# A two-layer retention and attention trunk: first stage in eight steps of 128 features, gates multiplied in the third group

## The chip, the cores and the metric

The kernel runs on one NeuronCore of a Trainium2 chip. The metric is the device time of one execution in microseconds (us); the time of a kernel is the median of its runs. The engines are TensorE (PE in the profile; its weight loads are PEld), VectorE (DVE), ScalarE (ACT), GpSimd (POOL) and SyncE (SP), which issues most loads. An engine works through its own queue in order.

## What is computed

One sequence of 512 tokens with 1024 features goes through two layers. Both begin with an RMS norm and a modulation from a condition vector, and end with a gated residual:

```python
cond = silu(c)
mod = cond @ ada_w[i] + ada_b[i]                 # 3 x 1024: shift, scale, gate
h = rms_norm(x, norm_g[i]) * (1 + scale) + shift
out = retention_mixer(h, ...) if i == 0 else chunked_attention_mixer(h, ...)
x = x + gate * out
```

Layer 0 (retention): `h @ w_in` gives q, k (4 heads of 256), v and a gate branch g (4 heads of 512); q and k are rotated by the positions (rope); scores with a decay, times v, RMS norm per head, times silu(g), then `@ w_out`. Layer 1 (attention): 16 heads of 128, RMS-normed q and k, softmax with a relative bias, times silu(g), then `@ w_out`. All is float32.

## The kernel before, in words

**Precision.** A float32 product is made of three fast ones: each operand is split into a high part (ScalarE, `AF.Copy` into float32r) and the rest (VectorE, source less high part); TensorE adds high x high, high x low and low x high. `split` (L305) does this for activations, `load` (L204) for weights: one load of 512 rows in a tile `raw`, the high part `whi`, the rest `wlo`. `nat_mm` (L226) and `tr_mm` (L235) issue the three matmuls for each 128 rows, with tokens or with features on the output's partitions.

**Condition and modulation.** `c_row` is loaded broadcast to 128 partitions (L76) and put through silu (L99). The 24 blocks of 128 rows of `ada_w` of a layer are loaded transposed; `ada_dot` (L123) takes the dot product of each row with the condition on VectorE (1024 columns at once). `ada_finish` (L128) adds the bias and makes the shift `sh`, the scale `gs`, or the gate: for the gate it spreads each value over the partitions by a product of a diagonal matrix with ones on TensorE (`diag` L145, `gp` L146) into `gates[layer]`.

**First stage (L348 to L398).** `norm_x` loads four x tiles of 128 tokens, normalises them (`norm_rows` L163: two squares on ScalarE, the mean and the power -0.5 on GpSimd in `rstd_of` L114, the scaling on VectorE, for the last tile on ScalarE), transposes them on TensorE and copies them to `xT`. `prepare(s)`, for four steps of 256 features, loads four blocks of `ada_w`, makes shift and scale, h on VectorE (L379) and its split, and loads and splits the weights of `first`: v of head 0 (rv0) and q of head 0 (rqk0_0), two thirds of head 0's q, k, v in all. The products of step s are issued behind `prepare(s + 1)`, into six accumulators of PSUM (pools `pm` and `pa`, four buffers each). The last step's products are issued behind `rope_tables` (L421), which makes `cos` and `sin` with some 14 operations on VectorE and two on ScalarE from the positions, loaded over GpSimd's queue (L423) into a buffer of the pool tag `nat`, which the h tiles of the stage use too. Then k of head 0 (rqk0_2) is a chunk of its own.

**The rest.** Work is cut into units of twelve matmuls of 512 columns. `go` (L294) issues units; `at` (L291) hangs other work behind a unit number: loads and dots of the remaining `ada_w` blocks (`side_load`, `side_dot`, L587 to L605: first the gate of layer 0 in units 2 to 16, then layer 1), scores and mixes (`hang_scores`, `hang_mix`). For each head of layer 0 come q and k, v, g; `out_proj` (L310) multiplies 512 features of the result with rows of `w_out` in four groups (`outp(0)` to `outp(3)`; a0 to a3 in layer 1). It scales the weights with the gate on GpSimd when they are loaded (L219, tile `raw_r` or `raw_a` of 512 rows by 512 columns) and adds the product to `xs` on VectorE (L327, L324). Behind the last group of layer 0 `done` (L629) hangs `norm_tile` (L184), the norm of layer 1. In the end the last group of layer 1 stores the result.

The order of each engine's queue is made by the tile framework's planner from the program's order and its own estimates, not written out by hand; `keep_in_program_order` pins the side loads and dots, `high_priority` the first silu.

## Time and profile before

| | us |
|---|---|
| median of 3 runs | 984.57 |
| the three runs | 982.72, 984.57, 985.76 |
| the profiled execution | 982.98 |
| its span in the profile | 981.2 |

Some 1.8 us of the profiled execution lie around its span. In a timeline a row gives the start, the duration, the engine, the line of the kernel, the operation with the tiles written and read, and in brackets how long the engine had idled and what released it. Matmuls are pipelined, so the distance between their starts is what one costs, not the printed duration. Short operations of VectorE overlap their neighbours in the same way.

### The profile page before, as it was taken

The page shows a single profiled execution, that of the slowest core. Times are in us where ns is not written, and L with a number is a line of the kernel's source. Part 1 is how long each engine was busy: PE and PEld are TensorE (multiplying, and loading weights), DVE is VectorE, ACT ScalarE, POOL GpSimd, SP SyncE. Part 2 cuts the span into 40 slices and gives each one's busy share as a digit, 9 for nine tenths or more (in the row PEclk, how much of TensorE's full clock was granted, in tenths as well). Part 3 has the DMA queues.
Part 4 walks back from the last instruction along what each step waited for, and adds up shares of the span by engine and source line. Part 5 has one row for each costly group of instructions (what it writes and reads, how often), then busy time and mean ns, then how long its engine had stood idle before and what let it go on. Part 6 is the DMA issues. An engine that isn't in the chain of part 4 may idle for free.

```text
span 981.2 us, 11783 instructions
## 1 busy us (share of the span) xinstructions
PE 949.3 (97%) x4528; PEld 793.6 (81%) x4528; DVE 601.1 (61%) x1023; ACT 373.8 (38%) x785; POOL 184.7 (19%) x169
## 2 busy tenths in 40 slices
PE   3889999999999999999999999999999999999997
PEld 2778888888888888778788888888878888888886
DVE  4977796568544775864455557444676346555674
ACT  6233322232233233354444445233543244444441
POOL 3000520051002012503001250002520012004410
PEclk8899999999999999999999999999999999999999
DMA  9654436434443433312333213223212232223202
GB/s 352 241 191 160 149 99 204 151 108 140 150 150 108 150 100 104 97 57 80 101 97 97 79 62 103 91 87 96 97 58 93 87 97 90 79 70 99 95 1 86
DMA packets 70296, 111.76 MB, mean 114 GB/s; under 512 B 11888, under 2 KB 36512, under 8 KB 70240
## 3 DMA queue, kind: packets, MB, share of 16 engines
q1 hardware_dynamic: 58256, 103.29, 31.5%
q0 software_dynamic: 10832, 5.62, 2.1%
q10 hardware_dynamic: 1152, 2.10, 0.6%
q8 instruction: 35, 0.57, 0.2%
q14 instruction: 21, 0.17, 0.1%
HBM read 108.83 MB, written 2.10 MB: 113 GB/s over the span
## 4 chain that ended last, share of the span: by engine, by line
PE 86%; DMA 4%; issue 4%; DVE 3%; ACT 1%; POOL 1%; SPq 0%; POOLq 0%; ACTq 0%; DVEq 0%
PE pm_aqk L233 5%; PE pm_aqk L231 5%; PE pm_aqk L232 5%; PE po_a L231 3%; PE po_a L233 3%; PE po_a L232 3%; PE pm_av L232 3%; PE pm_av L233 3%; PE pm_rg L239 3%; PE pm_rg L240 3%; PE ao L765 3%; PE as L725 3%; PE pm_av L231 3%; PE pm_rg L241 3%; PE ro L540 3%
## 5 line engine op out<-in xcount | busy, mean ns | idle before, releaser
L231 PE MATMUL pm_aqk<-whi_aqk,hTh 128*128 128x512 f32 x256 | 102.3, 400 | 1.1 <-ACT hTh L200 1.1
L233 PE MATMUL pm_aqk<-whi_aqk,hTl 128*128 128x512 f32 x256 | 100.4, 393 | 0.0
L232 PE MATMUL pm_aqk<-wlo_aqk,hTh 128*128 128x512 f32 x256 | 100.2, 391 | 0.0
L124 DVE CUSTOM_DVE_ANT_0 ada<-ada,cond 128x1024 f32<-128x1024 f32 x48 | 63.3, 1332 | 1.7 <-DMA ada<-in_ada_t_dram 1.7
L219 POOL TENSOR_TENSOR raw_r<-raw_r,gate 128x2048 f32<-128x2048 f32 x8 | 38.2, 4771 | 106.3 <-DMA raw_r<-in_ret_w_out_dram 92.9
L231 PE MATMUL pm_rv<-whi_rv,hTh 128*128 128x512 f32 x128 | 51.2, 407 | 6.7 <-ACT hTh L306 6.7
L231 PEld LDWEIGHTS pm_aqk<-whi_aqk,hTh 128*128 128x128 f32 x256 | 48.1, 188 | 10.9 <-ACT hTh L200 1.5
L233 PEld LDWEIGHTS pm_aqk<-whi_aqk,hTl 128*128 128x128 f32 x256 | 48.1, 188 | 10.6 <-DVE hTl L201 0.4
L232 PEld LDWEIGHTS pm_aqk<-wlo_aqk,hTh 128*128 128x128 f32 x256 | 48.2, 188 | 9.2
L734 ACT ACTIVATE p<-p,nm 128x128 f32<-128x128 f32 (+1 forms) x64 | 35.9, 563 | 48.7 <-DVE nm L732 47.6
L223 DVE TENSOR_TENSOR wlo_aqk<-raw_aqk,whi_aqk 128x2048 fp32r<-128x2048 f32 x16 | 36.6, 2290 | 28.0 <-ACT whi_aqk L222 28.0
L728 DVE CUSTOM_DVE_ANT_0 p<-as,br 128x128 f32<-128x128 f32 (+1 forms) x64 | 30.4, 486 | 36.9 <-PE as L725 34.0
L241 PE MATMUL pm_rqk<-hTh,wlo_rqk 128*128 128x512 f32 x128 | 49.7, 391 | 2.5 <-DVE wlo_rqk L223 2.5
L713 POOL DMA_DIRECT2D br<-in_att_bias_dram x16 | 13.4, 839 | 204.4 <-DVE nm L732 168.8
L232 PE MATMUL pm_rv<-wlo_rv,hTh 128*128 128x512 f32 x128 | 50.9, 402 | 0.0
L239 PE MATMUL pm_ag<-hTh,whi_ag 128*128 128x512 f32 x128 | 50.7, 397 | 0.0
L240 PE MATMUL pm_ag<-hTl,whi_ag 128*128 128x512 f32 x128 | 50.5, 394 | 0.0
L231 PE MATMUL po_r<-whi_r,yh 128*128 128x512 f32 x128 | 49.8, 391 | 0.5 <-ACT whi_r L222 0.5
L241 PE MATMUL pm_ag<-hTh,wlo_ag 128*128 128x512 f32 x128 | 50.2, 395 | 0.0
L233 PE MATMUL po_r<-whi_r,yl 128*128 128x512 f32 x128 | 50.1, 392 | 0.0
L232 PE MATMUL po_r<-wlo_r,yh 128*128 128x512 f32 x128 | 50.0, 391 | 0.0
L231 PE MATMUL pm_av<-whi_av,hTh 128*128 128x512 f32 x128 | 50.0, 391 | 0.0
(199 smaller groups left out, 2548.6 us busy)
## 6 DMA issues: line engine op xcount, KB each, us to landing
ada<-in_ada_t_dram SPq DMA_DIRECT2D x32, 512.0 KB, 4.4
raw_aqk<-in_att_w_in_dram SPq DMA_DIRECT2D x32, 512.0 KB, 4.6
ada<-in_ada_t_dram SPq DMA_DIRECT2D x8, 1024.0 KB, 13.8
raw_rg<-in_ret_w_in_dram SPq DMA_DIRECT2D x8, 1024.0 KB, 5.1
raw_r<-in_ret_w_out_dram SPq DMA_DIRECT2D x8, 1024.0 KB, 5.0
raw_ag<-in_att_w_in_dram SPq DMA_DIRECT2D x8, 1024.0 KB, 5.2
raw_av<-in_att_w_in_dram SPq DMA_DIRECT2D x8, 1024.0 KB, 5.1
raw_a<-in_att_w_out_dram SPq DMA_DIRECT2D x8, 1024.0 KB, 4.9
```

What stands on the lines that cost most here:

```text
L124: return nc.vector.tensor_tensor_reduce(raw, raw, cond, 1.0, 0.0, ALU.mult, ALU.add, mod[:, layer, block : block + 1])
L219: nc.gpsimd.tensor_tensor(raw, raw, scale.unsqueeze(1).broadcast_to([P, k1 - k0, width]), ALU.mult)
L223: nc.vector.tensor_tensor(lo, raw, f32(hi), ALU.subtract)
L231: nc.tensor.matmul(ps, a_h, wh[:, k, :], start=first and k == 0, stop=False)
L232: nc.tensor.matmul(ps, a_h, wl[:, k, :], start=False, stop=False)
L233: nc.tensor.matmul(ps, a_l, wh[:, k, :], start=False, stop=last and k == 3)
L239: nc.tensor.matmul(ps, wh[:, k, csl], h, start=first and k == 0, stop=False)
L240: nc.tensor.matmul(ps, wh[:, k, csl], l, start=False, stop=False)
L241: nc.tensor.matmul(ps, wl[:, k, csl], h, start=False, stop=last and k == 3)
L540: nc.tensor.matmul(ps[:, S - w :], a[:, fsl], b[:, psl], start=j == 0 and z == 0, stop=j == 3 and z == 2,)
L728: nc.vector.tensor_tensor_reduce(p[:, :w], ps[:, :w], br[:, S - w :], 1.0, -3.0e38, ALU.add, ALU.max, mx)
L734: nc.scalar.activation(p[:, :w], p[:, :w], AF.Exp, bias=nm, accum_out=sm)
```

## The change

What it does:

- The condition is loaded to one partition (ScalarE's queue), put through silu there, spread to 128 partitions by a matmul with ones, and copied back; a silu on a small tile `tick` stands ahead. The x tiles are first on SP's queue; the two small tables `ng` and `bt` move from GpSimd's queue to ScalarE's.
- `norm_rows` makes one of the two squares of the first norm on VectorE; the mean and epsilon are two small VectorE operations, only the power stays on GpSimd; all scaling is on VectorE.
- The first stage has eight steps of 128 features, holds v, q and k of head 0 in eight accumulators, makes h on ScalarE, adds the shift's bias on GpSimd, and has the rope tables behind its third step. The separate chunk of k is gone.
- The gate: groups 0 to 2 use unscaled weights. Group 0 writes `xs` (ScalarE), group 1 adds, group 2 adds, multiplies the sum with the gate and adds x, which it loads again (`again`). Group 3 has gate-scaled weights as before. For layer 1, `done` stores layer 0's result to a DRAM tile `x1` over GpSimd's queue. The dots of the side blocks are spread over units 4 to 93, and some work is hung two units later.

```diff
+    x1 = dp.tile([S, D], F32, name="x1")
...
-    nc.sync.dma_start(cond, c_row.broadcast_to([P, D]))
+    nc.scalar.dma_start(cond[0:1, :], c_row)
     xs = [cp.tile([P, D], F32, name=f"x_{t}") for t in range(NT)]
+    for t in range(NT):
+        nc.sync.dma_start(xs[t], x[t * P : (t + 1) * P, :])
...
     with tc.high_priority():
-        nc.scalar.activation(cond, cond, AF.Silu)
+        nc.scalar.activation(tick, tick, AF.Silu)
+    nc.scalar.activation(cond[0:1, :], cond[0:1, :], AF.Silu)
+    for half in range(2):
+        csl = slice(half * 512, (half + 1) * 512)
+        ps = pm.tile([P, 512], F32, tag="pm", name=f"cp_{half}")
+        nc.tensor.matmul(ps, ones[0:1, :], cond[0:1, csl], start=True, stop=True)
+        nc.scalar.activation(cond[:, csl], ps, AF.Copy)
...
-    def norm_rows(t, tag, scalar=False):
+    def norm_rows(t, tag, vector=False):
...
+            if vector and half:
+                nc.vector.tensor_tensor_reduce(
+                    xh, src, src, 1.0, 0.0, ALU.mult, ALU.add, ss[:, half : half + 1]
+                )
+            else:
+                nc.scalar.activation(xh, src, AF.Square, accum_out=ss[:, half : half + 1])
...
-        s1 = sp.tile([P, 16], F32, tag="s1", name=f"s1_{tag}_{t}")
-        nc.vector.tensor_tensor(s1[:, 0:1], ss[:, 0:1], ss[:, 1:2], ALU.add)
-        rs = rstd_of(s1[:, 0:1], D, 1)
+        ms = sp.tile([P, 2], F32, tag="s1", name=f"s1_{tag}_{t}")
+        nc.vector.tensor_scalar(ms[:, 0:1], ss[:, 0:1], 1.0 / D, EPS, ALU.mult, ALU.add)
+        nc.vector.scalar_tensor_tensor(
+            ms[:, 1:2], ss[:, 1:2], 1.0 / D, ms[:, 0:1], ALU.mult, ALU.add
+        )
+        rs = sp.tile([P, 1], F32, tag="rs", name="rs")
+        nc.gpsimd.tensor_tensor(rs, ms[:, 1:2], mhalf[:, 0:1], ALU.pow)
...
-    def out_proj(name, w_out, row0, ys, gate, store=None, t_outer=False, done=None, rstd=None):
+    def out_proj(name, w_out, row0, ys, gate, part, x_in, store=None, t_outer=False, done=None, rstd=None):
...
+        def again(half, tt):
+            xr[half, tt] = np_.tile([P, 2, 512], F32, tag="ada", name=f"xr_{name}_{half}_{tt}", bufs=2)
+            nc.sync.dma_start(
+                xr[half, tt],
+                x_in[tt * 256 : tt * 256 + 256, half * 512 : half * 512 + 512].rearrange(
+                    "(t p) n -> p t n", p=P
+                ),
+            )
         def unit(half, t):
+            if part == 2:
+                if half == t == 0:
+                    again(0, 0)
+                    again(0, 1)
+                elif (half, t) in ((0, 3), (1, 1)):
+                    again(1, half)
...
-                    [(ALLC, w_out[row0 : row0 + 512, csl])], f"{name}_{half}", scale=gate[:, csl],
+                    [(ALLC, w_out[row0 : row0 + 512, csl])], f"{name}_{half}",
+                    scale=gate[:, csl] if part == 3 else None,
...
+            rs = 1.0 if rstd is None else rstd()[:, t : t + 1]
+            acc = xs[t][:, csl]
+            if part == 0:
+                nc.scalar.activation(acc, ps, AF.Copy, scale=rs)
+            elif rstd is None:
+                nc.vector.tensor_tensor(acc, ps, acc, ALU.add)
             else:
+                nc.vector.scalar_tensor_tensor(acc, ps, rs, acc, ALU.mult, ALU.add)
+            if part == 2:
+                nc.vector.tensor_tensor(acc, acc, gate[:, csl], ALU.mult)
+                nc.vector.tensor_tensor(acc, acc, xr[half, t // 2][:, t % 2, :], ALU.add)
...
+    qk0 = [(slice(0, 256), 0), (slice(256, 512), D)]
     first = [
         Chunk("rv0", ret_w_in, [(ALLC, 2 * D)], False, None),
-        Chunk("rqk0_0", ret_w_in, [(h256, 0)], True, None, pa, "pa"),
+        Chunk("rqk0", ret_w_in, qk0, True, None, pa, "pa"),
     ]
...
+        wv = [[wp.tile([P, 4, 512], F32R, tag=a, name=f"{a}_rv0_{z}") for a in ("whi", "wlo")] for z in range(2)]
+        wq = [[st.tile([P, 4, 512], F32R, name=f"{a}_rqk0_{z}") for a in ("whi", "wlo")] for z in range(2)]
...
+        def prepare(kt):
+            raw = st.tile([P, 2, D], F32, tag="ada", name=f"ada_0_{kt}", bufs=3)
+            tc.keep_in_program_order(nc.sync.dma_start(raw, rows[kt]))
+            if kt % 2 == 0:
+                raws[0] = wp.tile([P, 4, 512], F32, tag="raw", name=f"raw_first_{kt}")
+            rw = raws[0][:, kt % 2 * 2 : kt % 2 * 2 + 2, :]
+            ksl = slice(kt * P, (kt + 1) * P)
+            nc.sync.dma_start(rw[:, 0, :], ret_w_in[ksl, 2 * D : 2 * D + 512])
             nc.sync.dma_start(
+                rw[:, 1, :].rearrange("p (g c) -> p g c", g=2), qk_in[ksl, :, 0:256]
+            )
+            ada_dot(raw[:, 1, :], 0, NK + kt)
+            g1, s1 = gs[:, 0, kt : kt + 1], sh[:, 0, kt : kt + 1]
+            nc.vector.scalar_tensor_tensor(
+                g1, mod[:, 0, NK + kt : NK + kt + 1], bt1[:, kt : kt + 1], ng[:, 0, kt : kt + 1],
+                ALU.add, ALU.mult,
+            )
+            ada_dot(raw[:, 0, :], 0, kt)
+            nc.gpsimd.tensor_tensor(s1, mod[:, 0, kt : kt + 1], bt[:, 0, kt : kt + 1], ALU.add)
+            half, k = divmod(kt, 4)
+            for (hi, lo), src in ((wv[half], rw[:, 0, :]), (wq[half], rw[:, 1, :])):
+                split(hi[:, k, :], lo[:, k, :], src)
+            h = np_.tile([P, S], F32, tag="p", name=f"h_0_{kt}", bufs=6)
+            nc.scalar.activation(h, xT[:, kt, :], AF.Identity, bias=s1, scale=g1)
+            split(hT["h"][:, kt, :], hT["l"][:, kt, :], h)
+
+        def products(kt):
+            for ch, w in zip(first, (wv, wq)):
+                ch.w = (None, *w[kt // 4])
+                for u in range(ch.n):
+                    ch.unit(kt // 4, u, range(kt % 4, kt % 4 + 1))
+
         prepare(0)
+        for kt in range(NK - 1):
+            prepare(kt + 1)
+            products(kt)
+            if kt == 2:
+                rope_tables()
...
-            u = 2 + 2 * z if z < 8 else 20 + (z - 8) * 7 // 2
+            u = 4 + z * 23 // 8
             at(max(u - 4, 0), side_load, layer, block)
             at(u, side_dot, layer, block)
-        rope_tables()
         for ch, ev in zip(first, (v_evac(0), qk_evac(0))):
             ch.evac = ev
-            for u in range(ch.n):
-                ch.unit(1, u, range(2, 4))
-        go(Chunk("rqk0_2", ret_w_in, [(h256, D)], True, qk_evac(0, 2)).units())
-        hang_scores(0, now[0] + 2)
+        products(NK - 1)
+        hang_scores(0, now[0] + 4)
...
-            hang_mix(n, u + 6)
+            hang_mix(n, u + 6 if n else u + 8)
...
         def done(t):
+            nc.gpsimd.dma_start(x1[t * P : (t + 1) * P, :], xs[t])
             at(now[0] + 1, norm_tile, 1, t)
...
-                gates[1], out if g == 3 else None, g == 3,
+                gates[1], g, x1, out if g == 3 else None, g == 3,
```

`rope_tables` itself and `rstd_of` for the attention's q and k are unchanged; the tables' tiles `cos` and `sin` come from a pool that is opened ahead of the stage.

## Rows read from the trace of the kernel before

**Rows 1.** The page, busy time: engine, us, share of the span, instructions.

```profile
PE 949.3 (97%) x4528; PEld 793.6 (81%) x4528; DVE 601.1 (61%) x1023; ACT 373.8 (38%) x785; POOL 184.7 (19%) x169
```

**Rows 2.** Waits of TensorE: waiter, whom it waited for, us in total, times, longest.

```profile
PE pm_rv L231 <- ACT hTh L306: 6.7, 2, 4.0
...
PE pm_rqk L241 <- DVE wlo_rqk L223: 2.5, 1, 2.5
PE pt L745 <- DVE p L737: 2.0, 2, 1.1
...
PE gp L146 <- DVE diag L145: 1.1, 1, 1.1
```

**Rows 3.** Timeline of TensorE: start us, us, what, [idle before <-releaser].

```profile
23.42 0.80 PE L231 MATMUL pm_rv<-whi_rv,hTh 128*128 128x512 f32 x1 [4.01 <-ACT hTh L306]
...
44.48 2.07 PE L231 MATMUL pm_rv<-whi_rv,hTh 128*128 128x512 f32 x4 [2.69 <-ACT hTh L306]
...
47.82 0.62 PE L239 MATMUL pm_rqk<-hTh,whi_rqk 128*128 128x512 f32 x2
...
75.36 0.39 PE L239 MATMUL pm_rqk<-hTh,whi_rqk 128*128 128x512 f32 x1
...
76.04 0.39 PE L239 MATMUL pm_rg<-hTh,whi_rg 128*128 128x512 f32 x1
```

**Rows 4.** Windows: PE, PEld, DVE, ACT, POOL busy us; PEclk granted; DMA share; GB/s.

```profile
20.00:25.00 5.00, 1.58 (x4) 1.29 (x5) 3.98 (x6) 3.42 (x6) 0.00 (x0) 0.50 1.03 409
30.00:35.00 5.00, 5.00 (x24) 4.14 (x23) 4.96 (x11) 1.15 (x2) 0.00 (x0) 1.00 1.02 414
```

**Rows 5.** DMA issues: what, queue, count, KB each, median us from issue to landing.

```profile
x<-in_x_dram SPq DMA_DIRECT2D x4, 512.0 KB, 7.4
...
posi<-in_positions_dram POOLq DMA_DIRECT2D x1, 256.0 KB, 8.1
```

**Rows 6.** Timelines of ScalarE, VectorE and GpSimd during the first normalisation.

```profile
5.22 1.06 ACT L99 ACTIVATE cond<-cond 128x1024 f32<-128x1024 f32 x1 [3.21 <-DMA cond<-in_c_row_dram]
...
12.72 0.62 ACT L168 ACTIVATE xn<-x 128x512 f32<-128x512 f32 x1
...
12.68 0.88 DVE L181 TENSOR_SCALAR xn<-x,rs 128x512 f32<-128x512 f32 x2 [0.44 <-POOL rs L119]
...
14.97 1.42 POOL L119 TENSOR_TENSOR rs<-ms,mhalf 128x1 f32<-128x1 f32 x1
```

**Rows 7.** Timeline of VectorE in the first stage.

```profile
23.67 0.69 DVE L307 TENSOR_TENSOR hTl<-h,hTh 128x512 fp32r<-128x512 f32 x1
24.27 1.22 DVE L124 CUSTOM_DVE_ANT_0 ada<-ada,cond 128x1024 f32<-128x1024 f32 x1
...
25.42 1.22 DVE L124 CUSTOM_DVE_ANT_0 ada<-ada,cond 128x1024 f32<-128x1024 f32 x1
...
55.70 0.43 DVE L429 CAST posf<-posi 128x512 f32<-128x512 int32 x1 [4.27 <-DMA posi<-in_positions_dram]
```

**Rows 8.** Groups of GpSimd by line: busy us, mean ns, idle before.

```profile
L219 POOL TENSOR_TENSOR raw_a<-raw_a,gate 128x2048 f32<-128x2048 f32 x8 | 38.5, 4809 | 20.5 <-DMA raw_a<-in_att_w_out_dram 10.6 <-DVE x L324 7.0 <-DVE ri L736 2.9
...
L713 POOL DMA_DIRECT2D br<-in_att_bias_dram x16 | 13.4, 839 | 204.4 <-DVE nm L732 168.8 <-DVE mx L728 35.5
```

**Rows 9.** Timeline of VectorE: one operation alone, three beside GpSimd's multiplications.

```profile
76.40 0.69 DVE L471 TENSOR_TENSOR rt<-rt,rt 128x512 f32<-128x512 f32 x1
...
135.70 5.10 DVE L471 TENSOR_TENSOR rt<-rt,rt 128x512 f32<-128x512 f32 x1
...
393.69 4.80 DVE L145 TENSOR_SCALAR diag<-ident,mod 128x128 f32<-128x128 f32 x2
...
711.25 4.72 DVE L737 TENSOR_SCALAR p<-p,ri 128x256 f32<-128x256 f32 x1
```

**Rows 10.** Windows of the third groups' stretches, columns as in rows 4.

```profile
384.00:416.00 32.00, 30.63 (x147) 25.39 (x145) 26.45 (x26) 10.85 (x10) 14.43 (x5) 1.00 0.32 99
923.00:950.00 27.00, 27.00 (x141) 22.87 (x140) 20.33 (x45) 10.55 (x21) 4.79 (x2) 1.00 0.12 39
```

More of the change, by code (lines that the diff above doesn't have):

```diff
@@ L87, in hybrid_trunk_kernel @@
     nc.gpsimd.dma_start(kg, att_kg_t)
-    ident = cp.tile([P, P], F32, name="ident")
-    make_identity(nc, ident)
     ones = cp.tile([P, P], F32, name="ones")
@@ L342, in hybrid_trunk_kernel, with rope_tables @@
     new_h(0)
-    h256 = slice(0, 256)
+    l0 = ExitStack()
+    tp = l0.enter_context(tc.tile_pool(name="tp", bufs=1))
+    cos = tp.tile([P, S], F32, name="cos")
+    sin = tp.tile([P, S], F32, name="sin")
+    def rope_tables():
+        posi = np_.tile([P, S], I32, tag="nat", name="posi")
+        nc.gpsimd.dma_start(posi, positions.broadcast_to([P, S]))
+        tiny = tp.tile([P, 64], F32, name="tiny")
+        ifr, hpi = tiny[:, 0:1], tiny[:, 1:2]
+        nc.gpsimd.dma_start(ifr, inv_freq)
+        nc.gpsimd.memset(hpi, math.pi / 2)
+        posf = np_.tile([P, S], F32, tag="nat", name="posf")
+        nc.vector.tensor_copy(posf, posi)
+        ang = np_.tile([P, S], F32, tag="nat", name="ang")
+        nc.vector.tensor_scalar(ang, posf, ifr, None, ALU.mult)
+        c1, c2, c3 = _two_pi_parts()
+        n1 = np_.tile([P, S], F32, tag="nat", name="n1")
+        n2 = np_.tile([P, S], F32, tag="nat", name="n2")
+        step = 2.0**11
+        nc.vector.tensor_scalar(n1, ang, 1.0 / (2 * math.pi * step), MAGIC, ALU.mult, ALU.add)
+        nc.vector.tensor_scalar(n1, n1, MAGIC, None, ALU.subtract)
+        for c in (c1, c2):
+            nc.vector.scalar_tensor_tensor(ang, n1, -c * step, ang, ALU.mult, ALU.add)
+        nc.vector.tensor_scalar(n2, ang, 1.0 / (2 * math.pi), MAGIC, ALU.mult, ALU.add)
+        nc.vector.tensor_scalar(n2, n2, MAGIC, None, ALU.subtract)
+        for c in (c1, c2, c3):
+            nc.vector.scalar_tensor_tensor(ang, n2, -c, ang, ALU.mult, ALU.add)
+        nc.vector.scalar_tensor_tensor(ang, n1, -c3 * step, ang, ALU.mult, ALU.add)
+        pi = float(np.nextafter(np.float32(math.pi), np.float32(0)))
+        nc.vector.tensor_scalar(ang, ang, pi, -pi, ALU.min, ALU.max)
+        nc.scalar.activation(sin, ang, AF.Sin)
+        nc.vector.scalar_tensor_tensor(n1, ang, -1.0, ang, ALU.mult, ALU.max)
+        nc.scalar.activation(cos, n1, AF.Sin, bias=hpi, scale=-1.0)
+    qk0 = [(slice(0, 256), 0), (slice(256, 512), D)]
     first = [
         Chunk("rv0", ret_w_in, [(ALLC, 2 * D)], False, None),
-        Chunk("rqk0_0", ret_w_in, [(h256, 0)], True, None, pa, "pa"),
+        Chunk("rqk0", ret_w_in, qk0, True, None, pa, "pa"),
     ]
@@ new lines, in hybrid_trunk_kernel @@
+        for t in range(NT):
+            xn = norm_rows(t, 0, True)
+            for half in range(2):
+                ps = pa.tile([P, 4, P], F32, tag="pa", name=f"hp_0_{t}_{half}")
+                for k in range(4):
+                    nc.tensor.transpose(ps[:, k, :], xn[half][:, k * P : (k + 1) * P], ident)
+                nc.scalar.activation(
+                    xT[:, half * 4 : half * 4 + 4, t * P : (t + 1) * P], ps, AF.Copy
+                )
+        rows = ada_t[0, : 2 * D].rearrange("(g q p) k -> q p g k", g=2, q=NK)
@@ new lines, in hybrid_trunk_kernel @@
+        qk_in = ret_w_in[:, : 2 * D].rearrange("k (g c) -> k g c", g=2)
+        raws = {}
+        def prepare(kt):
[6 more added lines that the diff above has]
+            nc.sync.dma_start(rw[:, 0, :], ret_w_in[ksl, 2 * D : 2 * D + 512])
@@ L373, in prepare @@
-        def prepare(s):
-            ada_256(NK + 2 * s)
-            ada_256(2 * s)
-            for kt in (2 * s, 2 * s + 1):
-                h = np_.tile([P, S], F32, tag="nat", name=f"h_0_{kt}")
-                nc.vector.tensor_scalar(
-                    h, xT[:, kt, :], gs[:, 0, kt : kt + 1], sh[:, 0, kt : kt + 1], ALU.mult, ALU.add
-                )
-                split(hT["h"][:, kt, :], hT["l"][:, kt, :], h)
-            for ch in first:
-                ch.load(s // 2, ks(s))
-        def ks(s):
-            return range(s % 2 * 2, s % 2 * 2 + 2)
@@ L389, in hybrid_trunk_kernel @@
-        norm_x()
-        prepare(0)
-        for s in range(3):
-            ws = [ch.w for ch in first]
-            prepare(s + 1)
-            for ch, w in zip(first, ws):
-                new, ch.w = ch.w, w
-                for u in range(ch.n):
-                    ch.unit(s // 2, u, ks(s))
-                ch.w = new
+            ada_dot(raw[:, 1, :], 0, NK + kt)
[4 more added lines that the diff above has]
+            )
@@ L411, in probabilities @@
         return pth, ptl
[L414 removed]
+    with l0:
         rp = l0.enter_context(tc.tile_pool(name="rp", bufs=1))
         pth, ptl = probabilities(rp)
[L418 to L449 removed]
         qk, vv, gg, pt, yy = {}, {}, {}, {}, {}
```

84 lines of the change are left out of this document (14 added, 70 removed).

## The prediction

> **What bounds the kernel now.** Read the busy line of the page first: TensorE is busy for 949.3 of 981.2 us [rows 1], so only idle time, slow matmuls and the start can be won. The waits of TensorE say how much idle time there is and who ends it [rows 2]: behind the first normalisation, the largest entries are the two waits of pm_rv for hTh (6.7 us), one for wlo_rqk (2.5), two for p (2.0), one for diag (1.1). Then the timeline of TensorE gives their places [rows 3]: the first product starts at 23.42, after 4.01 us of waiting; the second wait of pm_rv (2.69) ends at 44.48; the first matmul of pm_rg, which marks the end of the 192 matmuls of rv0 and of head 0's q and k, is at 76.04. Three matmuls from 75.36 to 76.04 give 0.227 us each at the full clock; eight from 44.48 to 47.82 give 0.42, and the first ten behind 23.42 start as far apart. The windows say why: the granted clock is 0.50 in 20 to 25 us, that is 1.2 GHz, and 1.00 in 30 to 35 [rows 4]. So ten cold matmuls cost 10 x 0.2 = 2.0 us, and this was paid twice.
>
> The 192 matmuls need 43.6 us at full clock. From 23.42 to 76.04 there are 52.6: 43.6 + 4.0 cold + 2.7 + 2.5 of waits accounts for it.
>
> **The start.** Before it come 2 MB of x, normalisation, transposes, two rows of dots and a split. The broadcast load of the condition (512 KB, as much as an x tile) stood ahead of x on SP's queue; it becomes 4 KB on ScalarE's queue. At the 414 GB/s of a saturated window [rows 4] that brings the last x tile 1.27 us forward. Behind it the last square ended at 13.3 and GpSimd's power only at 16.4 [rows 6], 7.0 us ahead of the first product. One of the two GpSimd steps goes to VectorE, h goes to ScalarE, and weight splits halve. Counted from VectorE instead, which now has a square, a scaling pair and two tiny operations for each of four tiles (0.60 + 0.88 + 0.3), then two dots of 1.15 (the distance of two dots in [rows 7]): 7.1 + 2.3 = 9.4 us, from the first x tile, which takes the place of the condition's load (landed at 5.22 [rows 6]), gives 14.6; with a GpSimd addition (up to the 1.42 of [rows 6]), h, split and some gaps, a first product near 17.9. The spread of the condition (two matmuls, two copies) lies in the wait for x and costs nothing; if x came 4 us sooner it would be on the path. Gain 5.5 us; bounds 3.5 (GpSimd's steps stay at 1.4) and 7.5 (all gaps close).
>
> **The eight steps.** Each step has 24 matmuls, 5.45 us. VectorE does two dots and three splits of 512 columns (0.60 apart [rows 7]): 2.3 + 1.8 + 0.2 = 4.3. A step loads 1.57 MB, 3.8 us at 414 GB/s, so neither loads nor VectorE is slower than TensorE, and the 2.69 us wait and the second cold stretch (2.0) should go. The rope tables move in: 14 VectorE operations between 0.43 and 0.69 us [rows 7, 9], some 8. VectorE's 8 x 4.3 + 8 = 42.4 against TensorE's 43.6: the cover is nearly used up. Before, the tables waited 4.27 us for the positions [rows 7], whose load takes 8.1 [rows 5], and this pushed the weight split that TensorE waited 2.5 for [rows 2]. The buffers that held that load back are no longer used by the stage, so I drop the 2.5, and charge 1.0 (0 to 4.3: the same wait again, with every dot and split behind it in VectorE's queue).
>
> **The end of the stage.** All evictions now come at once: 20 VectorE operations (v splits, rotation, q and k splits), 12 us at 0.60, and rg's weight split of 2048 columns, 2.4. Scores are hung four units on, 48 matmuls or 10.9 us. Before, the q half was turned ahead of k. I charge 1.0 (0 to 3.5). Head in all: -5.5 - 2.7 - 2.0 - 2.5 + 1.0 + 1.0 = -10.7, so pm_rg at about 65.3.
>
> **The gate multiplications.** Sixteen GpSimd multiplications scale output weights, eight in each layer; those of layer 1 take 4.8 us [rows 8]. Twelve go. Beside one, VectorE stands still: a tensor_tensor that takes 0.69 alone took 5.10 at 135.70, two diagonals 4.80 at 393.69, a scaling of p 4.72 at 711.25 [rows 9]. The last two gave TensorE its waits for diag and one of those for p: with a1's multiplication gone and the last diagonals earlier, -1.1 and -1.1. Part 0 goes to ScalarE (38% busy), at no cost; were that queue full, some 0.6 a unit, as its squares take [rows 6]. The dots are spread over 93 units; their number is the same, and no wait of TensorE names them.
>
> What is added: in the third group of each layer 16 VectorE operations (gate, then x again), 16 x 0.60 = 9.6 us, and 2 MB loaded on SP's queue, which has room there. In layer 0 they fall into 384 to 416 us, where VectorE is busy for 26.5 of 32, in layer 1 into 923 to 950, 20.3 of 27 [rows 10]: some 4 and 3 us too much. Queued behind them are r3's evictions, and in layer 1 the last softmaxes, for which TensorE waits. And the four remaining gate multiplications stand just there: each can hold an added operation for up to 4.8. Four accumulators (10.9 us) cover layer 0: +1.0 (0 to 5). The end of layer 1 has less cover: +2.5 (0 to 8). Storing x1 adds four issues to GpSimd's queue ahead of the norms' power; they lie beside the squares: nothing, or, without that cover, 0.84 each, as GpSimd's other issues take [rows 8].
>
> The Trainium skill's page "SBUF — State Buffer", section "Who interferes with whom", says that a VectorE instruction with two SBUF inputs is shut out by a GpSimd instruction that reads SBUF, not merely slowed. The 5.10 us row agrees; by that rule the added operations, all with two SBUF inputs, meet the upper ends of the two charges, 984.7 in all.
>
> **Sum.** Span 981.2 - 10.7 - 2.2 + 1.0 + 2.5 = 971.8. The profiled run has 982.98 for a span of 981.2, and stands 1.6 under the median 984.57, so in terms of the median 984.6 - 9.4 = 975.
>
> **Rivals.** (a) All cover holds and no charge falls due, start at the early end: -7.5 - 7.2 - 2.2, about 968. For it: VectorE idles 4.3 us in the old stage; against: its sum is within 1.2 us of TensorE's. 0.17.
> (b) VectorE becomes the bound of the stage: tables in one run ahead of step 4, and waiting 4.3 for positions. The stage gains some 5 only: 984.6 - 5 - 2.2 + 3.5 = 981. 0.13.
> (c) The late additions meet the lock at both ends, +5 and +8: 984.6 - 10.7 - 2.2 + 13 = 984.7, no change. 0.09.
> (d) Slower: the pieces are too short. A step waits in itself (load, dots, GpSimd's addition, ScalarE's two passes, split) and if VectorE's order leaves no step ready ahead, TensorE idles about 2.7 us before each of seven steps and then runs ten matmuls at 1.2 GHz, as at 44.48: 7 x 4.7 = 33 us. Stage end 17.9 + 43.6 + 2.0 + 33 = 96.5, 20 later than now; with the late terms 984.6 + 20.5 + 1.3 = 1006. It decides only where a step's inputs come later than the 5.45 us of the step before. For it: exactly that happened once, at 44.48; against: there each piece held twice the work for VectorE, and 4.3 is below 5.45. 0.07.
> The Trainium skill's page "TensorE: Matmul & The Clock Gate", section "HAM oscillation — how this bites in real kernels", describes such a kernel, with short bursts between waits, throttled again at every one. The row at 44.48 agrees for one wait; no run here shows it for many.
>
> **Chances.** The forecast, 970 to 980, has 0.54, with (a) 0.17, (b) 0.13, (c) 0.09, (d) 0.07. A difference under 0.3% (3 us) can't be told from none here. Faster: 0.54 + 0.17 + most of (b) = 0.81; same: (c) and the rest of (b), 0.11; slower: (d) and a little of (c), 0.08. The range of 8 in 10 goes from (a)'s 967 to 982, past (b).
>
> **What would show it.** Right: first product at 16 to 20 us, one cold stretch, no TensorE wait over 2 us until pm_rg near 65; no waits at gp and one fewer at pt; posf not waiting for positions; VectorE nearly full in the old 384 to 416 and 923 to 950 stretches. Wrong: granted clock under 1.00 at step starts (d), waits for hTh or wlo between steps with VectorE full (b), or waits for p, ay or po late in a layer with VectorE operations of 4 to 5 us (c).

## The result, and the profile after

The changed kernel takes 991.46 us in the median (990.95 to 993.12), the kernel before 985.16 in the same measurement: ratio 1.0081, 95% interval 1.0058 to 1.0103. It is slower, by 6 us in the medians and 8 in the profiled spans (981.2 to 989.2 us), where 975 was forecast.

The page's busy line [rows 1]: TensorE is busy for 10.4 us longer, and VectorE and GpSimd for less.

```profile
span 989.2 us, 11875 instructions
PE 959.7 (97%) x4532; PEld 797.9 (81%) x4532; DVE 585.5 (59%) x1052; ACT 388.7 (39%) x808; POOL 125.2 (13%) x160
```

The waits of TensorE (total, times, longest, us):

```profile
PE hp L438 <- DVE xn L200: 4.5, 2, 3.3
PE pm_rg L258 <- DVE vl L326: 4.2, 1, 4.2
...
PE pm_rv L250 <- ACT hTh L325: 2.9, 1, 2.9
PE po_a L251 <- DVE wlo_a L242: 2.2, 1, 2.2
PE po_r L250 <- DVE x L368: 2.1, 2, 1.1
PE po_r L251 <- DVE wlo_r L242: 2.0, 1, 2.0
PE qt L723 <- DVE qn L715: 1.7, 1, 1.7
PE pt L797 <- DVE p L789: 1.0, 1, 1.0
```

Against [rows 2] the forecast's removals happened: pm_rv waits for hTh once, at the start, and not between steps; the waits of pm_rqk and gp are gone, and one of p's. In their place stand one new wait of 4.2 us at pm_rg, and four at po_r and po_a that end on VectorE. The timeline of TensorE has the places [rows 3]:

```profile
22.67 0.80 PE L250 MATMUL pm_rv<-whi_rv,hTh 128*128 128x512 f32 x1 [2.94 <-ACT hTh L325]
...
69.35 0.40 PE L260 MATMUL pm_rqk<-hTh,wlo_rqk 128*128 128x512 f32 x1
74.00 0.80 PE L258 MATMUL pm_rg<-hTh,whi_rg 128*128 128x512 f32 x1 [4.25 <-DVE vl L326]
...
415.21 0.47 PE L250 MATMUL po_r<-whi_r,yh 128*128 128x512 f32 x1 [1.10 <-DVE x L368]
419.51 0.50 PE L250 MATMUL po_r<-whi_r,yh 128*128 128x512 f32 x1 [1.03 <-DVE x L368]
424.78 0.50 PE L251 MATMUL po_r<-wlo_r,yh 128*128 128x512 f32 x1 [1.97 <-DVE wlo_r L242]
```

The windows of TensorE at the end of the stage (PEclk is the column behind POOL):

```profile
65.00:70.00 5.00, 4.75 (x21) 3.55 (x19) 2.24 (x4) 2.13 (x2) 0.14 (x1) 1.00 0.00 0
70.00:75.00 5.00, 1.00 (x2) 0.83 (x3) 5.00 (x8) 2.91 (x6) 0.98 (x2) 0.73 0.26 37
75.00:80.00 5.00, 5.00 (x15) 3.94 (x14) 5.00 (x10) 0.24 (x2) 0.14 (x1) 0.58 0.68 215
```

Read together: the first product comes 0.75 us earlier, and from there to the last of the 192 matmuls it takes 46.9 us instead of 52.6, so the eight steps work. But then TensorE stands for 4.25 us and starts again at 1.2 GHz (granted clock 0.73 and 0.58 in the two windows): the twelve matmuls from 74.00 to 79.24 stand 0.44 us apart instead of 0.227, which costs 2.5 us. Matmuls at this lower clock are called cold below. So the start at 74.00 is worth one at 76.5 at full clock, no better than the 76.04 of the kernel before. Places that all kernels here have cut the span into parts (us):

| kernel | first product | first pm_rg | pm_rg to last po_r | last po_r to last po_a | span |
|---|---|---|---|---|---|
| before | 23.42 | 76.04 | 360.8 | 539.7 | 981.2 |
| after | 22.67 | 74.00 | 368.7 | 541.9 | 989.2 |
| e1, gates alone | 23.04 | 75.01 | 366.1 | 542.0 | 988.6 |
| e12, gates behind group 2 | 22.47 | 72.87 | 362.6 | 538.7 | 978.7 |
| e13, the same on before | 22.95 | 75.34 | 358.7 | 538.6 | 977.2 |
| e16, best | 19.78 | 65.93 | 360.9 | 537.9 | 969.4 |

So layer 0 behind the stage lost 7.9 us, of which 2.5 are the cold matmuls, and layer 1 lost 2.2; both numbers are net of the waits for gp and for one p that went, 1.1 in each layer.

### The profile page after: what moved, and what is told of

Read it like the earlier page. It is cut to its first block, busy times and chain, and to the rows that moved or that the text cites. A ratio compares the mean times of both kernels' runs of the same rounds, so it can differ in the third digit from the quotient of the medians.

```text
span 989.2 us, 11875 instructions
## 1 busy us (share of the span) xinstructions
PE 959.7 (97%) x4532; PEld 797.9 (81%) x4532; DVE 585.5 (59%) x1052; ACT 388.7 (39%) x808; POOL 125.2 (13%) x160
## 4 chain that ended last, share of the span: by engine, by line
PE 88%; DVE 6%; DMA 2%; issue 1%; POOL 1%; ACT 0%; SPq 0%; POOLq 0%; DVEq 0%
PE pm_aqk L250 5%; PE pm_aqk L251 5%; PE pm_aqk L252 5%; PE ro L594 3%; PE pm_rg L258 3%; PE pm_rv L250 3%; PE pm_rg L259 3%; PE pm_rv L251 3%; PE pm_rg L260 3%; PE pm_rqk L258 3%; PE pm_rv L252 3%; PE pm_av L251 3%; PE ao L817 3%; PE pm_av L250 3%; PE pm_av L252 3%; PE pm_rqk L259 3%
## 5 line engine op out<-in xcount | busy, mean ns | idle before, releaser
L139 DVE CUSTOM_DVE_ANT_0 ada<-ada,cond 128x1024 f32<-128x1024 f32 x48 | 58.0, 1218 | 5.3 <-DMA ada<-in_ada_t_dram 5.3
L258 PE MATMUL pm_rg<-hTh,whi_rg 128*128 128x512 f32 x128 | 51.1, 399 | 4.2 <-DVE vl L326 4.2
L715 DVE TENSOR_TENSOR qn<-pm_aqk,rs 128x512 f32<-128x512 f32 x32 | 22.1, 689 | 51.6 <-POOL rs L134 51.3
L259 PE MATMUL pm_rg<-hTl,whi_rg 128*128 128x512 f32 x128 | 51.0, 398 | 0.0
L260 PE MATMUL pm_rg<-hTh,wlo_rg 128*128 128x512 f32 x128 | 50.8, 397 | 0.0
L259 PE MATMUL pm_ag<-hTl,whi_ag 128*128 128x512 f32 x128 | 50.6, 396 | 0.0
L260 PE MATMUL pm_ag<-hTh,wlo_ag 128*128 128x512 f32 x128 | 50.6, 395 | 0.0
L252 PE MATMUL po_r<-whi_r,yl 128*128 128x512 f32 x128 | 50.6, 395 | 0.0
L258 PE MATMUL pm_ag<-hTh,whi_ag 128*128 128x512 f32 x128 | 50.6, 396 | 0.0
```

The lines of the kernel that those rows point to most:

```text
L139: return nc.vector.tensor_tensor_reduce(raw, raw, cond, 1.0, 0.0, ALU.mult, ALU.add, mod[:, layer, block : block + 1])
L252: nc.tensor.matmul(ps, a_l, wh[:, k, :], start=False, stop=last and k == 3)
L258: nc.tensor.matmul(ps, wh[:, k, csl], h, start=first and k == 0, stop=False)
L259: nc.tensor.matmul(ps, wh[:, k, csl], l, start=False, stop=False)
L260: nc.tensor.matmul(ps, wl[:, k, csl], h, start=False, stop=last and k == 3)
```

## The experiments

Times are medians, with the ratio to the kernel before as measured beside each. The changed kernel was measured at another time than these runs. Differences to it are of medians; by the ratios it stands 1.4 to 2.4 us further above every run than by the medians.

### The two halves alone

`e1_gate_alone`: the kernel before with the new out_proj, its calls, the copy x1 and the new spread.

```diff
-                    [(ALLC, w_out[row0 : row0 + 512, csl])], f"{name}_{half}", scale=gate[:, csl],
+                    [(ALLC, w_out[row0 : row0 + 512, csl])], f"{name}_{half}",
+                    scale=gate[:, csl] if part == 3 else None,
...
-            u = 2 + 2 * z if z < 8 else 20 + (z - 8) * 7 // 2
+            u = 4 + z * 23 // 8
```

> The kernel before with the second half of the change alone: gates on the accumulated groups, x loaded again, the dots respread; the first stage is that of before. My theory (the late additions meet the lock of GpSimd's remaining multiplications in both layers): slower than before by 4 to 8 us, 989 to 993 in the median; TensorE's excess over 0.227 us a matmul grows by about 4 us in 400 to 480 us and by about 3.5 behind 920, while the waits for gp and one for p (2.2) go. Rival (the gate change is neutral and the first stage alone makes the loss): within 2 us of before, 983 to 987.

990.02 us, ratio 1.0046 (1.0031 to 1.0060): the gates alone make the kernel slower by 4.5 us. What the stage adds to that is 1.4 us by the medians and 3.4 by the ratios, whose intervals touch; it gains nothing, at any rate.

`e2_stage_alone`, and later `e11_gates_before`: the reverse, the stage with all weights multiplied by GpSimd. e2 packs the gate's dots tighter; e11 has the spread of before and both ends of the stage mended (below).

```diff
-                    scale=gate[:, csl] if part == 3 else None,
+                    scale=gate[:, csl],
...
-            u = 4 + z * 23 // 8
+            u = 2 + z * 10 // 7 if z < 8 else 16 + (z - 8) * 7 // 2    # e2
+            u = 2 + 2 * z if z < 8 else 20 + (z - 8) * 7 // 2          # e11
```

> The changed kernel with the gates as before: all output weights scaled by GpSimd, x not loaded again. My theory (the stage gains about 6 us by 69 us and loses as much at its end; the tails cost the rest): within 2 us of before, 983 to 987, with pm_rg at 75 to 77 as in both kernels, and the tail's excess back at that of before (about 4 us in 400 to 480, 1.7 behind 920). Rival (the stage alone makes the loss): 990 or more.

> Both orders mended, with the gates and the spread of the dots as in the kernel before: GpSimd multiplies all sixteen weights, nothing is added to VectorE. My theory (the mended stage keeps its 8 us; GpSimd's multiplications take back 2 to 7 of it where they fall on evictions that TensorE waits for, as at 144 us in the run with the stage alone): 977 to 982, slower than with the gates behind the second group. Rival (the 11 us of the run with the stage alone come from the stage itself): 988 or more.

996.33 us (1.0112, 1.0097 to 1.0128) and 989.08 (1.0040, 1.0026 to 1.0054). My theory missed both, and the rivals' numbers came, but for the most part not by the stage itself. In e2 a multiplication falls on the evictions of k (rows of GpSimd, VectorE and TensorE), and the scores wait 2.72 us:

```profile
141.50 5.05 POOL L237 TENSOR_TENSOR raw_r<-raw_r,gate 128x2048 f32<-128x2048 f32 x1 [2.50 <-ACT gate L162]
...
141.46 5.64 DVE L325 TENSOR_TENSOR kl<-rt,kh 128x512 fp32r<-128x512 f32 x2
...
147.16 0.51 PE L562 MATMUL st<-qh,kl 128*128 128x512 f32 x1 [2.72 <-DVE kl L325]
```

With the cold matmuls behind it TensorE loses 5.6 us in 120 to 160 us, of the 13.3 by which the span of e2 stands over that of before. In e11 the first output group comes while the second half of layer 0's gate is still being made: GpSimd waits for the gate until 145.47, TensorE for the weights until 152.02. With the cold matmuls behind it TensorE loses 10 us in 120 to 160. This execution, the slowest of e11's eight, also has a late third x tile (first product at 22.79) and a wait of 1.59 us between two steps.

```profile
145.47 4.55 POOL L239 TENSOR_TENSOR raw_r<-raw_r,gate 128x2048 f32<-128x2048 f32 x1 [20.34 <-ACT gate L162]
...
152.02 0.79 PE L251 MATMUL po_r<-whi_r,yh 128*128 128x512 f32 x1 [7.25 <-ACT whi_r L242]
```

The dots hang on units, and the stage took its units out of that count. So the two halves are tied: an earlier stage needs gates that are due later.

### The two ends of the stage

At the end, ScalarE's and VectorE's timelines of the changed kernel:

```profile
66.99 1.92 ACT L241 ACTIVATE whi_rg<-raw_rg 128x2048 fp32r<-128x2048 f32 x1 [7.93 <-PE pm_rv L252]
69.78 2.07 ACT L325 ACTIVATE vh<-pm_rv 128x512 fp32r<-128x512 f32 x4 [0.88 <-PE pm_rqk L260]
...
70.19 2.28 DVE L242 TENSOR_TENSOR wlo_rg<-raw_rg,whi_rg 128x2048 fp32r<-128x2048 f32 x1
...
73.26 0.68 DVE L326 TENSOR_TENSOR vl<-pm_rv,vh 128x512 fp32r<-128x512 f32 x1
```

vh reads only pm_rv, but is released by the last product of pm_rqk. vh's tiles belong to a pool that takes the memory of the stage's pool, where the q and k weights lie. Behind it, vl, which frees the accumulator for pm_rg, comes after a split of 2.28. Two runs take this apart.

`e3_qk_first`:

```diff
-            for ch, w in zip(first, (wv, wq)):
+            pairs = list(zip(first, (wv, wq)))
+            for ch, w in pairs[::-1] if kt == NK - 1 else pairs:
```

> The changed kernel, the last of the eight steps with the q and k products ahead of those of v, nothing else. My theory (the eviction of v waits for the last q/k product, because its tiles lie where the q/k weights lay, and so holds the accumulator that rg's first matmul wants): the 4.25 us wait of pm_rg falls under 1, the cold matmuls behind it (about 2 us) go, pm_rg stands near 70, and the time falls by 4 to 6.3 us, to 985 to 987.5. Rival (VectorE's queue is what holds v's eviction: 12 us of evictions, the split of rg's weights among them, ahead of it): the wait stays at 3 to 5 us, the time within 1.5 us of the changed kernel.

986.81 us, 1.0010 (1.0000 to 1.0020): 4.65 less than the changed kernel. The wait fell to 0.4, pm_rg to 70.21. But VectorE's queue changed too, so memory was tested by itself:

`e14_swap_memory`:

```diff
-        wv = [[wp.tile([P, 4, 512], F32R, tag=a, name=f"{a}_rv0_{z}") for ...
-        wq = [[st.tile([P, 4, 512], F32R, name=f"{a}_rqk0_{z}") for ...
+        wv = [[st.tile([P, 4, 512], F32R, name=f"{a}_rv0_{z}") for ...
+        wq = [[wp.tile([P, 4, 512], F32R, tag=a, name=f"{a}_rqk0_{z}") for ...
```

> The changed kernel, the first stage's weights of v and of q and k change their places in memory (v's in the stage's own pool, q's and k's in the weight buffers), nothing else; v's products still come ahead of q's and k's. My theory (v's evictions wait for the last q/k product because their tiles lie where the q/k weights lay): the eviction starts at about 67 instead of 69.78, the 4.25 us wait of pm_rg falls under 1 and the cold matmuls behind it go, as when the products change places; 985 to 988 in the median, less what the second half of rg's weights now waits for (0 to 2). Rival (the order of VectorE's queue alone, the split of rg's weights ahead of v's): the wait stays at 3 us or more, time within 1.5 us of the changed kernel.

984.50 us, 0.9994 (0.9979 to 1.0009), a little better than expected. vh now starts on its own product (ScalarE's timeline):

```profile
67.83 2.07 ACT L325 ACTIVATE vh<-pm_rv 128x512 fp32r<-128x512 f32 x4 [7.68 <-PE pm_rv L252]
```

No wait of pm_rg is left, and the granted clock is 1.00 from 60 to 80. Memory was the cause. The queue's order followed from it: VectorE's splits of v moved ahead of that of rg's weights as well, though only the memory was changed.

At the start, VectorE's timeline of the changed kernel shows two dots (L139) and two weight splits between the mean of the last x tile (L192) and its scaling (L200):

```profile
12.53 0.15 DVE L192 TENSOR_SCALAR s<-ss 128x1 f32<-128x1 f32 x1
13.11 1.23 DVE L139 CUSTOM_DVE_ANT_0 ada<-ada,cond 128x1024 f32<-128x1024 f32 x1 [0.43 <-DMA ada<-in_ada_t_dram]
...
15.41 0.15 DVE L193 SCALAR_TENSOR_TENSOR s<-ss,s 128x1 f32<-128x1 f32 x1
...
17.16 0.87 DVE L200 TENSOR_SCALAR xn<-x,rs 128x512 f32<-128x512 f32 x2
```

`e4_norm_first`:

```diff
+            scaled[0] = nc.vector.tensor_scalar(xn[half], src, rs, None, ALU.mult)
...
-        prepare(0)
+        with tc.issue_after(scaled[0].ins):    # the last scaling of x
+            prepare(0)
```

> The changed kernel with one order put on VectorE's queue: the dots of the first step come behind the last normalisation of x, nothing else. My theory (two dots and two casts stand ahead of the last tile's scaling in VectorE's queue): the first product starts at 18 to 19.5 instead of 22.67, and pm_rg comes as much earlier, so the time falls by 3 to 4.5 us. Rival (the dots only change places with the normalisation: VectorE's sum to the first h is the same, and the first product waits for h instead): first product at 21 to 23, time within 1.5 us of the changed kernel.

988.98 us, 1.0040 (1.0027 to 1.0053): 2.5 less than the changed kernel, between the two theories (by the ratios 4.0, in the range of mine); the first product, at 21.04, is where the rival had it. The scaling now ends at 15, but then the dots and two splits stood ahead of the scale of h.

### The ends of the layers

`e6_all_mended` is e3 and e4 together, and the base of the next three.

> The changed kernel with both orders mended: the dots of the first step behind the last normalisation, and the q and k products of the last step ahead of those of v; the gates stay in the third group. My theory (two losses in the first stage that have nothing to do with each other): the gains of the two runs add up, 4.6 and 2.5, so 984 to 985. Rival (the earlier stage runs into GpSimd's work or into late loads, as the run with the gates of before did at 144 us): less than 5 us of gain, 986.5 or more.

984.79 us, 0.9999 (0.9983 to 1.0014), as expected: the two ends add up.

`e8_no_lock` and `e9_no_adds` don't compute the output. e8 leaves the gate out of the last group's weights, so GpSimd multiplies no weights at all; e9 leaves gate and x out of the first three groups, the second load of x with them:

```diff
-                    scale=gate[:, csl] if part == 3 else None,
+                    scale=None,                                        # e8
...
-            if part == 2:                                              # e9
-                nc.vector.tensor_tensor(acc, acc, gate[:, csl], ALU.mult)
-                nc.vector.tensor_tensor(acc, acc, xr[half, t // 2][:, t % 2, :], ALU.add)
```

> Both orders mended, and the last group's output weights are not multiplied by the gate, so this part of the computation is left out and GpSimd has no multiplication of weights at all. My theory (VectorE's standstill beside GpSimd is the larger part of what the tails lose): 4 to 7 us less than with both orders mended. Rival (the number of VectorE operations is what costs): within 2 us of it.

> Both orders mended, and the sixteen added VectorE operations of each layer (gate, then x) and the second load of x are left out, so gate and residual are missing from the first three groups; GpSimd still multiplies the last group's weights. Both theories: the tails' excess goes back to that of before or lower, 6 to 9 us less than with both orders mended; the difference is the whole price of the added operations, lock included. If it is under 3 us, the tails' loss is neither.

975.18 us (0.9912, 0.9895 to 0.9928) and 973.04 (0.9893, 0.9876 to 0.9910): 9.6 and 11.75 less than e6, both more than expected. What TensorE takes over 0.227 us a matmul of 512 columns (narrower ones counted by their own distance), its excess, is 8.6 us in 400 to 480 and 5.3 behind 920 in the changed kernel; it is some 2.6 and 1.8 with the additions alone (e8), and as much with the multiplications alone (e9). So the pair costs some 9.5 more than either part. What a part costs by itself isn't known beyond these 4.4, as no run leaves out both. The timelines of the changed kernel show them meet, GpSimd's first, then VectorE's, as before in [rows 9]:

```profile
396.55 5.91 POOL L238 TENSOR_TENSOR raw_r<-raw_r,gate 128x2048 f32<-128x2048 f32 x1 [4.14 <-ACT sq L603]
...
404.11 5.08 POOL L238 TENSOR_TENSOR raw_r<-raw_r,gate 128x2048 f32<-128x2048 f32 x1
...
400.08 2.92 DVE L370 TENSOR_TENSOR x<-x,gate 128x512 f32<-128x512 f32 x1
...
404.63 5.10 DVE L370 TENSOR_TENSOR x<-x,gate 128x512 f32<-128x512 f32 x1
```

And VectorE's groups by line put a number on it, sixteen gate operations in the changed kernel and in e8 (busy us, mean ns):

```profile
L370 DVE TENSOR_TENSOR x<-x,gate 128x512 f32<-128x512 f32 x16 | 20.4, 1277 | 0.0
```

```profile
L372 DVE TENSOR_TENSOR x<-x,gate 128x512 f32<-128x512 f32 x16 | 10.9, 687 | 0.1
```

These operations stand 9.5 us longer beside the multiplications. That this is about what e8 gained can be chance, as not all of VectorE's time is TensorE's.

`e7_gate_second`, on e6's base, `e12_gate_second_alone`, on the changed kernel, and `e13_gate_second_old`, on e1's: gate and x go on one group earlier, since groups 3 and 4 follow each other without a pause and 1 and 2 don't.

```diff
-                    scale=gate[:, csl] if part == 3 else None,
+                    scale=gate[:, csl] if part > 1 else None,
...
-            if part == 2:
+            if part == 1:
                 nc.vector.tensor_tensor(acc, acc, gate[:, csl], ALU.mult)
```

> Both orders mended, and gate and x go on behind the second group of each layer instead of the third; GpSimd multiplies the weights of groups 3 and 4 (four a layer instead of two). The sixteen added VectorE operations of a layer then lie in its middle, where VectorE is half busy. My theory (the added operations cost because groups 3 and 4 follow each other without a pause at the end of a layer): the excess in 400 to 480 and behind 920 falls back to that of before, 6 to 8 us less than with both orders mended alone, plus 0 to 2 for two more multiplications in each tail: 977 to 981. Rival (GpSimd's multiplications are what costs, wherever the additions stand): 984 to 988.

> The changed kernel with gate and x behind the second group instead of the third, nothing else: the two orders of the first stage stay as in the changed kernel. My theory (the tails lose about 10 us wherever the stage ends): 980 to 983, about 10 under the changed kernel. Rival (the gain needs the earlier stage, as the collisions shift with it): 985 or more.

> The kernel before with gate and x behind the second group of each layer alone, the first stage as before. My theory (twelve, now eight, multiplications of GpSimd fewer, nothing added where VectorE is full): the waits for gp and for one p (2.2 us) go, 981 to 983.5. Rival (the added operations meet GpSimd's multiplications in the middle as well): 985 or more.

974.66 us (0.9903, 0.9885 to 0.9920), 981.60 (0.9962, 0.9949 to 0.9975) and 976.86 (0.9922, 0.9909 to 0.9936). e7 came 2 us under its range. VectorE's gate operations have a mean of 688 ns again in e7, with twice as many multiplications on GpSimd. On the changed kernel one group earlier is worth 10 us, as expected. On the old stage it turns a loss of 4.5 into a gain of 7.5, some 4 us more than I had expected: TensorE's excess in 360 to 440 us is 0.4, against 3.8 before, so more than the wait for gp went.

The same three runs price the stage, by the ratios: as made it costs 3.9 us (e12 against e13), with both ends mended it gains 1.9 (e7 against e13, whose intervals overlap), and 5.1 in e16 below.

### The start again, and the last step

`e10_h_first`, on e7:

```diff
-            nc.vector.scalar_tensor_tensor(
+            last = nc.vector.scalar_tensor_tensor(
...
+            with tc.issue_after(last.ins) if kt == 0 else ExitStack():    # the scale of h
                 for (hi, lo), src in ((wv[half], rw[:, 0, :]), (wq[half], rw[:, 1, :])):
```

> Both orders mended and the gates behind the second group, and in the first step VectorE makes the scale of h ahead of the two weight splits, so that ScalarE has h and its rounding ahead of the next step's weights. My theory (the first product waits for a chain through two queues, not for loads): first product at 19.3 to 20 instead of 20.95, the time 0.8 to 1.6 us under that of the gates behind the second group with both orders mended. Rival (behind the first product the steps are bound by VectorE, so an earlier start is given back): within 0.5 us of it, with a TensorE wait between two steps.

973.39 us, 0.9886 (0.9871 to 0.9902); first product at 19.50. Both numbers as expected.

`e15_swap_h_gate`: e10 with the exchange of memory in place of the exchange of products.

> Gates behind the second group, the dots behind the last normalisation, h's scale ahead of the weight splits, and the weights' places in memory exchanged instead of the order of the last products. My theory (the memory is what the end of the stage waits for, and with v's eviction at once the next weights come in time as well): the 1.1 us wait of pm_rg that was left goes, 972 to 973.2. Rival (rg's second weights now wait for the last q/k product, and the exchange gives back what it saves): 973.4 or more, with a wait of pm_rg for wlo_rg or whi_rg.

973.36 us, 0.9892 (0.9865 to 0.9919), undecided: three times from 971.0 to 971.7 and three from 975.1 to 976.7. The profiled execution is one of the upper three. pm_rg doesn't wait, but TensorE waits in the last step (its timeline, then GpSimd's, then VectorE's), where e10, with the same operations of VectorE around it, shows the row behind:

```profile
57.41 0.80 PE L252 MATMUL pm_rv<-whi_rv,hTh 128*128 128x512 f32 x1 [3.11 <-ACT hTh L327]
...
51.81 4.18 POOL L462 TENSOR_TENSOR sh<-mod,bt 128x1 f32<-128x1 f32 x1 [2.92 <-DVE mod L139]
...
51.93 0.67 DVE L408 SCALAR_TENSOR_TENSOR ang<-n,ang 128x512 f32<-128x512 f32 x1
52.53 2.27 DVE L244 TENSOR_TENSOR wlo_rg<-raw_rg,whi_rg 128x2048 fp32r<-128x2048 f32 x1
54.73 1.21 DVE L139 CUSTOM_DVE_ANT_0 ada<-ada,cond 128x1024 f32<-128x1024 f32 x1
```

```profile
52.02 0.24 POOL L462 TENSOR_TENSOR sh<-mod,bt 128x1 f32<-128x1 f32 x1 [2.92 <-DVE mod L139]
```

An addition of 128 values stands for 4.18 us, until VectorE has done a rope operation, a split of 2048 columns and a dot. The same addition takes 4.17 or 4.18 us in the traces of e4, e6, e8 and e11 too, and 0.24 in those of e7 and e9. What it costs TensorE there goes from nothing (e8) to the 1.59 us of e11. `e16_shift_scalar` takes it off GpSimd, and `e17_shift_scalar_order` does so in e10:

```diff
-            nc.gpsimd.tensor_tensor(s1, mod[:, 0, kt : kt + 1], bt[:, 0, kt : kt + 1], ALU.add)
+            nc.scalar.activation(s1, mod[:, 0, kt : kt + 1], AF.Identity, bias=bt[:, 0, kt : kt + 1])
```

> The kernel before this one (gates behind the second group, both ends of the stage mended, weights exchanged in memory), with the addition that makes the shift of h in each step (128 values) on ScalarE instead of GpSimd. My theory (its last addition stands on GpSimd for 0.24 us in one execution and 4.18 in another behind the same VectorE operations, and where it stands long, TensorE waits 3.1 us for hTh and runs cold behind it): the upper of the two groups of times (975.1 to 976.7) goes and the lower (971.0 to 971.7) stays, median 970.8 to 971.8. Rival (the wait for hTh comes from late loads or from VectorE's fullness): times of both groups, median 972.5 or more.

> The same addition moved to ScalarE in the kernel with the exchanged order of the last products (weights' places in memory as in the changed kernel). My theory: its single time of 976.7 goes, the others stay: median 972.8 to 973.5, all within 1 us of each other. Rival: no change in the spread.

971.14 us (0.9870, 0.9851 to 0.9890; four of five between 971.0 and 971.3, one 974.5) and 972.85 (0.9881, 0.9865 to 0.9896; 972.5 to 973.8). None of e16's times lies in the upper group, where e15 had three of six; the cause of the 974.5 no profile shows. The first product to pm_rg takes 46.2 us in e16 and 50.6 in e15's profiled execution, so the row accounts for the distance of the groups, though no execution of e15's lower group was profiled. e17 shows little: e10 had one high time in five, and four without one can be luck; they spread over 1.2 us, where I had expected 1. e16 is the fastest kernel: 1.3% under the kernel before, 2.1% under the changed one. Its waits of TensorE behind the first product:

```profile
PE qt L721 <- DVE qn L713: 1.2, 1, 1.2
PE pt L795 <- DVE p L787: 0.9, 1, 0.9
```

## Why the prediction was wrong

Three terms of the sum failed: the start, the end of the stage, and the charge for the gates in layer 0.

**The start.** 17.9 was forecast, 22.67 came, and 19.50 with both orders mended. The sum was of VectorE's own work from the first x tile, and took for granted that its queue holds that work in the order of need. It holds dots and splits ahead of the last scaling; this step failed. Mended (e10), 1.6 us remain. VectorE idles for 3.6 us between the first x tile and the end of the second dot, for x tiles, a small table and powers, which the sum left out; an x tile 0.9 us earlier than taken (4.32 against 5.22) and a shorter way from the dots to the product make up for 2.0 of it.

**The eight steps.** Right: one wait at the start, none between steps, the position load hidden, both waits of [rows 2] and the second cold stretch gone. Rival (d) is refuted in the changed kernel, though e15 and e11 show its wait, behind GpSimd's addition, for one step each. Rival (b) is refuted too, as VectorE idles for 9.5 us up to 67.76, before the stage ends. The rope tables' 1.0 wasn't needed. A cold stretch costs more than I had read: the rows of before show eight matmuls far apart behind 23.42, not ten, but in the changed kernel there are twelve, 2.5 us, each time.

**The end of the stage.** Charged 1.0 (0 to 3.5), measured 4.25 of waiting and 2.5 for the cold matmuls. The term counted VectorE's evictions and looked for the next user of a tile by its data; this step failed. What set the end was the next user of its memory (e14). The start came 4.8 us late and the end cost 5.8 more than charged, the rest is right but for small terms: the head, in full-clock terms, lost 0.5 instead of gaining 10.7. The forecast of pm_rg near 65.3 was reached by e16, at 65.93.

**The gates.** The waits for gp and one p went, -2.2, as forecast. What the late place costs is read between two kernels with the same stage, the changed one and e12: 368.7 - 362.6 = 6.1 us in layer 0, of which 0.8 is a shorter cold stretch behind pm_rg in e12's execution, and 541.9 - 538.7 = 3.2 in layer 1. So the charge of 1.0 in layer 0 came out at 5.3, a little past its upper end of 5, and this step failed; that of 2.5 in layer 1 came out at 3.2, within its ends. I had put four accumulators in front of layer 0's additions as cover, but the third and the fourth group follow each other, and VectorE, held for 6.7 us in the two rows of 2.92 and 5.10 (0.68 without a multiplication), never catches up there. Rival (c) had the mechanism right, and its 13 for both ends was too much: 8.5 by these spans. The Trainium skill's page "SBUF — State Buffer", section "Who interferes with whom", by whose rule I had named the upper ends, says that the order of issue decides which of the two engines is shut out. The 1277 against 687 ns agree for VectorE. The 4.18 us of e15 can be the reverse case, but that row starts 0.12 us ahead of the first of the three VectorE instructions that it covers, and the page speaks of one instruction.

**The sum.** 981.2 + 0.5 (head) + 5.4 (layer 0 behind the cold matmuls) + 2.1 (layer 1) = 989.2. The 5.4 and the 2.1 hold some 1.8 and 1.2 us that aren't the gates' (below). That the steps would work and their gain be lost at the start and the end was in none of the rivals, and the range, made from them, ended at 982.

**Open.** From pm_rg to the last po_r the new stage's kernels with gates behind group 2 and no cold stretch take 360.9 to 361.0 us, the old stage's 358.7, with the same matmuls at the same clock and no wait over 0.4 us. Most of these 2 us lie in the matmuls of po_r. The 38 from the first of the second group on, in the kernel before and then in the changed one, where nothing was added to this group yet but an unscaled weight:

```profile
232.86 0.39 PE L231 MATMUL po_r<-whi_r,yh 128*128 128x512 f32 x1
...
241.25 0.39 PE L232 MATMUL po_r<-wlo_r,yh 128*128 128x512 f32 x1
```

```profile
233.96 0.40 PE L250 MATMUL po_r<-whi_r,yh 128*128 128x512 f32 x1
...
242.56 0.39 PE L251 MATMUL po_r<-wlo_r,yh 128*128 128x512 f32 x1
```

That is 0.2268 and 0.2324 us a matmul. Unbroken ones have a mean of 0.232 in every kernel with the new stage and of 0.227 to 0.228 in the three with the old one (before, e1, e13), whatever the gates: 1.8 us for the 384 of layer 0. Those of po_a have 0.231 against 0.228, 1.2 us. So this is a cost of the stage that no term of mine held, and why it arises no run shows.

Profiled executions stand mostly up to 2 us off their medians, on either side, and e6's 5 above, so differences of that size are read from the ratios. In e6's the granted clock fell behind the three waits of some 2 us at the ends of the layers (near 419, 473 and 955 us), where the changed kernel's stayed at 1.00.

## What to carry to other kernels

When a stage ends sooner, ask for each eviction behind it not only what it reads but what lay in the memory that it writes, and where the planner's order puts it in its engine's queue: both can hold a finished accumulator. Work that is moved off GpSimd onto VectorE pays here only where it doesn't land beside what stays on GpSimd: with the same sixteen operations a layer, the old stage's kernel took 7.5 us less than before with them one group earlier, though GpSimd then kept twice as many multiplications, and 4.5 more with them at the end of a layer. And a part of a change that fails as made can be right: price each part alone and in another place before dropping it.

## What the runs showed of the hardware that I had not expected

A tiny GpSimd operation can stand through several VectorE instructions in a row: 4.17 to 4.18 us for 128 values in five of the kept traces, 0.24 in three, with the same VectorE operations around it in e15 and e10. That this made e15's two groups of times is likely from e16, and not shown beyond it.

And two kinds of work that meet, each of which alone left TensorE an excess of some 4.4 us at the ends of the layers, left 13.9 together: a price taken with the other part missing says little of the pair.
